# Decoder step with three token mixers on one core: first projection phase in written order with evictions ahead of the next splits, and a new layout of the kernel's end

## Chip, cores, metric

One core of one Trainium2 chip. The metric is the device time of one execution in microseconds (us). Before the change it was 1824.22 us, the median of 3 runs (1823.52 to 1826.77).

## What is computed

One layer of a hybrid decoder is applied to a prompt of 256 positions and to 8 samples of one position each (264 columns in all, width 2048, everything in fp32):

```python
mod = silu(c) @ w_ada + b_ada;  sh1, sc1, gt1, sh2, sc2, gt2 = split(mod, 6)
h = rmsnorm(x, g_pre_mix) * (1 + sc1) + sh1
z = h @ w_in                      # u, v, HGRN2 and GLA inputs, branch gates
...                               # three mixers, gated merge -> merged
x = x + gt1 * rmsnorm(merged @ w_out, g_post_mix)
h2 = rmsnorm(x, g_pre_mlp) * (1 + sc2) + sh2
y2 = square(relu(h2 @ w_mlp_up)) @ w_mlp_down
x = x + gt2 * rmsnorm(y2, g_post_mlp)
```

## The kernel before

**Splits.** Activations and weights are split into a rounded high part and a rest. Each product of a 128x128 weight tile with the 264 columns is three matmuls (L659, L660, L661): high weights times high x, high weights times low x, low weights times high x. `split` (L108) makes the parts of a weight half-tile: ScalarE casts (`whi`, L109), VectorE subtracts (`wlo`, L106). A **granule** (L649) is the work on one item of the weight stream, 8 weight tiles in the first phase, so 24 matmuls. The stream loads items on SyncE's queue (L616, L609; 4 raw buffers) up to five ahead, and `ahead()` splits up to two items ahead of the granule in work; `granule` calls it when its matmuls have been written.

**First phase** (L809 to L844). x has 16 blocks of 128 rows (k). `CHUNKS = (2, 2, 4, 4, 4)` deals them out in five **k steps**, numbered 0 to 4 here. Each k step runs over all twenty 256-column pieces of u, v, q, f and i (`begin`): in k steps 0 and 1 a granule has two pieces (accumulators acc0 and acc1 in PSUM, 12 matmuls each) and there are ten granules, 0 to 9; later there are twenty of one piece. When a granule is done, its accumulators are evicted: copied to SBUF by ScalarE in k step 0 (L825), added to what lies there by VectorE in the others (L827). There are two accumulator buffers, so a granule's acc0 needs the eviction of the last granule's acc0, and acc1 that of acc1.

**What runs ahead.** While k step c runs, `First.paced` loads the columns of `w_ada` that make the shift and scale of k step c+1, on GpSimd's queue (L488; sixteen loads, of 256 KB in k step 0 and of 512 KB after), and spreads their small matmuls (`ada`, L308) behind granules 3 to 6 or so. ScalarE copies the sums (L312), TensorE transposes them, VectorE adds the bias into `mod` (L509) and makes `A1` (L515). Then `modulate` (L439) forms x * A1 + shift: for the samples' 16 columns on VectorE (L451, L452), on GpSimd for the first blocks alone (L445); for the prompt, of each two blocks the first on VectorE (L456), the second on ScalarE (L458). The result is split (`split_tokens`, L121) into the high and low x that the next k step's matmuls read.

**Order.** In the first phase, TensorE, SyncE and GpSimd run in written order (`manual_schedule`, L807); VectorE's and ScalarE's instructions are put in order by the framework's scheduler. Every engine carries out its own list in order, so an instruction that waits holds up all behind it.

**The end** (L1637 to L1710). The last product of the MLP, its eighth column pair (m = 7, L1638 to L1653), goes into both halves of one accumulator. `gated` (L1413) squares it for the norm and multiplies by the gate; four transposes bring it to token order (L851) and two copies (L1447, L1448) put it into the output rows `yt`. Three of the eight 128x512 output pieces are made on TensorE (`by_pe`, L1671): x1 times the identity (L1681), then yt times a diagonal of the norm factors (L1690), both into one accumulator, read out by ScalarE (L1696). The sums of squares (`norms`, L1463, L1464) stand behind two of the L1681 matmuls. A square root on ScalarE (L228) and five small VectorE operations (L229 to L233) give the norm factors `r3`. VectorE makes the other five pieces (L1698). The samples' rows take two VectorE operations (L1703, L1704), a transpose, a copy and a store on ScalarE's queue (L1709). Stores of pieces alternate between SyncE's and ScalarE's queues.

Of the kernel before, what the change touches and what calls it, by code (L numbers as in the profile page):

```python
# [10 lines left out]
AF = mybir.ActivationFunctionType  # L11
# [46 lines left out]
def hybrid_step_kernel(  # L58
# [40 lines left out]
    def mul(o, a, b):  # L99
        V.tensor_tensor(o, a, b, op=ALU.mult)  # L100

    def add(o, a, b):
        V.tensor_tensor(o, a, b, op=ALU.add)  # L103
# [335 lines left out]
    def modulate(dst, src, xs, k0, n, A, B, hi, lo):  # L439

        d = dst[:, :, NP:NT]
        one = k0 == 0
        if one:
            Q = nc.gpsimd
            Q.tensor_tensor(d, xs[:, k0:k0 + n, :], A[:, k0:k0 + n, 1:NC], op=ALU.mult)  # L445
            Q.tensor_tensor(d, d, B[:, k0:k0 + n, 1:NC], op=ALU.add)
            hs, ls = (apart(b)[:, :, :, NP // 2:NT // 2] for b in (hi, lo))
            Q.tensor_copy(hs, by_two(d))
            Q.tensor_tensor(ls, by_two(d), hs.bitcast(F32), op=ALU.subtract)
        else:  # L450
            mul(d, xs[:, k0:k0 + n, :], A[:, k0:k0 + n, 1:NC])  # L451
            add(d, d, B[:, k0:k0 + n, 1:NC])  # L452
        for j in range(n):
            k = k0 + j
            if j % 2 == 0:
                V.tensor_scalar(dst[:, j, 0:NP], src[:, j, :], A[:, k, 0:1], B[:, k, 0:1], ALU.mult, ALU.add)  # L456
            else:
                S.activation(dst[:, j, 0:NP], src[:, j, :], AF.Identity, scale=A[:, k, 0:1], bias=B[:, k, 0:1])  # L458
            if one:
                p = by_two(dst[:, j:j + 1, 0:NP])  # L460
                h, l = (apart(b[:, j:j + 1, :])[:, :, :, 0:NP // 2] for b in (hi, lo))
                if j == 0:
                    V.tensor_copy(h, p)
                    sub(l, p, h.bitcast(F32))
                else:
                    split(p, h, l)
            elif j % 2 == 1:
                js = slice(j - 1, j + 1)
                split_tokens(dst[:, js, :], hi[:, js, :], lo[:, js, :])
# [176 lines left out]

    stream = []

    def granule(w, k0, n, c0, width, accs, xh, xl, k, first, last):  # L649

        item, parts = stream[0].next()
        assert item[1:] == (k0 + k, n, c0, width)
        h = n // 2
        for acc0, m0 in [(acc, 2 * i) for i, acc in enumerate(accs)]:
            for j in range(n):
                for m in range(m0, min(m0 + 2, width // P)):
                    o = acc0[:, m % 2, 0:NT]
                    a, b = (p[:, j % h, m * P:(m + 1) * P] for p in parts[j // h])
                    T.matmul(o, a, xh(k + j), start=first and j == 0, stop=False)  # L659
                    T.matmul(o, a, xl(k + j), start=False, stop=False)  # L660
                    T.matmul(o, b, xh(k + j), start=False, stop=last and j == n - 1)  # L661
        stream[0].ahead()

    levels, samples = [], []
# [138 lines left out]
    stream[0].split_half(0)  # L803
    for k, ps in zip((4, 6), early):
        x_transposed(k, ps)
    order.__exit__(None, None, None)
    order = tc.manual_schedule(engines=set(every[0:3]))  # L807
    order.__enter__()
    k0 = 0  # L809
    for ci, n in enumerate(CHUNKS):  # L810
        final = ci == len(CHUNKS) - 1
        gn = 4 // n
        ng = len(begin) // gn
        if not final:
            nxt = First(k0 + n, CHUNKS[ci + 1]).paced(ng)
        for gi in range(ng):
            if ci or gi:
                accs = [new_acc() for _ in range(gn)]
            else:
                next(nxt)  # L820
            granule(win, 0, n, begin[gi * gn][0], gn * CW, accs, hH, hL, k0, True, True)
            for acc, (c0, dst, fn) in zip(accs, begin[gi * gn:gi * gn + gn]):
                z = acc[:, :, 0:NT]
                if ci == 0:
                    S.copy(dst, z)  # L825
# [810 lines left out]

    def down(f, ah, al):  # L1637
        for m in range(8):  # L1638
            z = linear(w_mlp_down[0], f * (FB // P), FB // P, m * CW, CW, ah, al)
            dst = pair(y2[m // 2], m % 2)  # L1640
            if f == 0:
                S.copy(dst, z)
            elif f < NFB - 1 or m < 7:
                add(dst, dst, z)
            else:
                for i in range(2):
                    add(dst[:, i, :], dst[:, i, :], z[:, i, :])
            if f == NFB - 1:
                g = gated(m, dst, G2)
                if m < 7:  # L1650
                    later.append((now[0], lambda m=m, g=g: put_rows(m, to_tokens(g), yt)))
                else:
                    return g  # L1653

    zs = begin_up()
    order.__exit__(None, None, None)
# [3 lines left out]
    for f in range(NFB):  # L1660
        nxt = up(f + 1) if f + 1 < NFB else None
        if f == NFB - 1:
            rounds.drain()
            mul(G2, mod[:, 5 * KT:6 * KT, :], gpost2T.unsqueeze(2).to_broadcast([P, KT, NC]))
            yt = [[blk([P, 1024]) for _ in range(2)] for _ in range(2)]
        g = down(f, *pend)
        pend = nxt

    by_pe = [(0, 1, 0), (1, 1, 0), (1, 0, 0)]  # L1671
    acc = new_acc()
    sums_pe = {}

    def piece(rows, t, hf, c0):
        return rows[t][hf][:, c0:c0 + 512]

    pt = to_tokens(g)
    for i, p in enumerate(by_pe):
        sums_pe[p] = acc[:, i, :] if i < 2 else sm()  # L1680
        T.matmul(sums_pe[p], ident, piece(x1, *p), start=True, stop=False, skip_group_check=True)  # L1681
        if i == 1:
            r3 = norms()
    put_rows(7, pt, yt)
    r3s = r3[:, 2:2 + NS]
    dg = tmp([P, 2, P], "vt")
    for t in range(2):
        S.activation(dg[:, t, :], ident, AF.Copy, scale=r3[:, t:t + 1])
    for p in by_pe:
        T.matmul(sums_pe[p], dg[:, p[0], :], piece(yt, *p), start=False, stop=True, skip_group_check=True)  # L1690
    for t in range(2):
        for hf in range(2):
            for c0 in (0, 512):
                y = piece(yt, t, hf, c0)
                if (t, hf, c0) in by_pe:
                    S.copy(y, sums_pe[t, hf, c0])  # L1696
                else:
                    V.scalar_tensor_tensor(y, y, r3[:, t:t + 1], piece(x1, t, hf, c0), ALU.mult, ALU.add)  # L1698
                eng = nc.sync if c0 else nc.scalar
                eng.dma_start(y_prompt[0, t * P:(t + 1) * P, hf * 1024 + c0:hf * 1024 + c0 + 512], y)  # L1700
            if t == 0 and hf == 0:
                ys = tmp([P, NS, KT], "sqs", 1)
                mul(gs, gs, r3s.unsqueeze(1).to_broadcast([P, KT, NS]))  # L1703
                add(ys.rearrange("p b k -> p k b"), gs, xsT)  # L1704
                ps = sm([P, P])
                T.transpose(ps, ys.rearrange("p b k -> p (b k)"), ident)
                yo = tmp([P, P], "xsn", 1)
                S.copy(yo, ps)
                nc.scalar.dma_start(y_sample.rearrange("b o (k p) -> (b o k) p", p=P), yo)  # L1709
    order.__exit__(None, None, None)  # L1710


# [45 lines left out]
```

## Time and profile before

| | |
|---|---|
| runs, median (lowest to highest) | 1824.22 us (1823.52 to 1826.77) |
| profiled execution | 1827.14 us |
| its span | 1825.4 us, granted clock 0.996 |
| TensorE busy | 98% of the span |
| VectorE, ScalarE, GpSimd busy | 65%, 55%, 7% |
| HBM | 241 GB/s over the span |

The span is the stretch between the first and last recorded instruction; 1.7 us of the profiled execution lie around it. A timeline row gives start, duration, engine, line, operation and tiles, and in brackets how long the engine had been idle and what it was released by. A row of waits gives engine, tile and line, the releaser, then total us, number and longest. A matmul's record (0.28 us) is longer than the distance between two matmuls, since they are pipelined. "PEld" is the loading of weights, "SPq", "ACTq" and "POOLq" the issuing of DMAs.

### The profile page before, as it was taken

Reading aid. Unit: us, or ns where it says so; the run is one execution under the profiler, and the core shown is the slowest. Engines: PE = TensorE matmul, PEld = TensorE weight load, DVE = VectorE, ACT = ScalarE, POOL = GpSimd, SP = SyncE. Lnnn points to the kernel's source line nnn. Section 1 sums busy time; section 2 is a strip of 40 time slices with the busy share of each in tenths; the row PEclk is TensorE's granted clock in tenths of the full one; section 3 lists DMA queues with packets and bytes.
Section 4 is the critical chain, followed back from the end, with each engine's and each line's share of the span. In section 5 each row is a group of like instructions: output and inputs, shape, how many; then the busy total and the mean of one; then the engine's idle time right before and its main releaser. Section 6 shows DMA issues by size and latency. Waiting matters only on the chain.

```text
span 1825.4 us, 42105 instructions
## 1 busy us (share of the span) xinstructions
PE 1780.2 (98%) x16964; PEld 1690.1 (93%) x16964; DVE 1181.2 (65%) x2092; ACT 1001.2 (55%) x1827; POOL 132.3 (7%) x211
## 2 busy tenths in 40 slices
PE   6999999999999999999999999999999999999998
PEld 4889999989989998989999989999999999999997
DVE  4566677787677696566555667555666666666666
ACT  5444364676766766655444666554554545454554
POOL 4221100102101111210000000000000000000000
PEclk9999999999999999999999999999999999999999
DMA  9999687688788789897988954777666666666663
GB/s 317 360 332 313 197 300 236 210 257 284 239 283 261 236 271 299 264 326 244 305 252 266 330 167 153 250 255 221 196 197 196 196 194 196 193 196 196 196 197 106
DMA packets 330179, 442.05 MB, mean 242 GB/s; under 512 B 14946, under 2 KB 276944, under 8 KB 329984
## 3 DMA queue, kind: packets, MB, share of 16 engines
q1 hardware_dynamic: 311728, 380.26, 65.1%
q0 software_dynamic: 17184, 57.85, 9.1%
q8 instruction: 133, 2.18, 0.5%
q10 hardware_dynamic: 1072, 1.25, 0.2%
q14 instruction: 62, 0.51, 0.1%
HBM read 427.60 MB, written 11.70 MB: 241 GB/s over the span
## 4 chain that ended last, share of the span: by engine, by line
PE 87%; DMA 2%; DVE 2%; issue 2%; ACT 1%; POOL 0%; DVEq 0%; ACTq 0%; POOLq 0%
PE mm L659 27%; PE mm L661 26%; PE mm L660 26%; PE ada L376 3%; DMA vbc<-vs_d 1%; PE ada L308 1%; DVE wlo L106 1%; PE sm L851 1%; DMA raw<-in_w_in_dram 1%; PE sm L679 1%; PE sm L686 0%; DVE b L106 0%; PE sm L1575 0%; DMA st<-in_state_hgrn_dram 0%; DVE b L100 0%
## 5 line engine op out<-in xcount | busy, mean ns | idle before, releaser
L659 PE MATMUL mm<-b,whi 128*128 128x264 f32 x4624 | 1292.7, 280 | 11.7 <-ACT b L825 3.6
L661 PE MATMUL mm<-b,wlo 128*128 128x264 f32 x4624 | 1279.4, 277 | 5.3 <-DVE wlo L106 5.0
L660 PE MATMUL mm<-b,whi 128*128 128x264 f32 x4624 | 1278.8, 277 | 1.9 <-issue 1.1
L106 DVE TENSOR_TENSOR wlo<-raw,whi 128x512 fp32r<-128x512 f32 x1136 | 774.5, 690 | 487.7 <-ACT whi L109 475.8
L109 ACT CAST whi<-raw 128x512 fp32r<-128x512 f32 x1136 | 691.4, 616 | 645.7 <-DVE wlo L106 332.0
L659 PEld LDWEIGHTS mm<-b,whi 128*128 128x128 f32 x4624 | 876.0, 189 | 53.9 <-issue 26.6
L661 PEld LDWEIGHTS mm<-b,wlo 128*128 128x128 f32 x4624 | 876.0, 189 | 7.1 <-DVE wlo L106 7.1
L660 PEld LDWEIGHTS mm<-b,whi 128*128 128x128 f32 x4624 | 876.3, 190 | 2.9 <-issue 1.2
L103 DVE TENSOR_TENSOR b<-b,mm 128x528 f32<-128x528 f32 (+1 forms) x137 | 95.7, 699 | 24.5 <-PE mm L661 12.9
L1106 DVE SCALAR_TENSOR_TENSOR st<-vbc,b,st 128x128 f32<-128x128 f32 (+1 forms) x96 | 34.2, 391 | 52.7 <-DMA vbc<-vs_d 47.5
L1104 ACT ACTIVATE st<-st,fs 128x128 f32<-128x128 f32 (+1 forms) x96 | 37.0, 429 | 46.3 <-DMA st<-in_state_hgrn_dram 27.8
L488 POOL DMA_DIRECT2D b<-in_w_ada_dram x64 | 46.3, 726 | 126.9 <-PE ada L308 94.4
L376 PE MATMUL ada<-araw,cT 128*32 128x512 f32 x296 | 39.8, 601 | 0.0
L308 PE MATMUL ada<-b,cT 128*32 128x256 f32 (+1 forms) x640 | 34.6, 351 | 2.7 <-DMA b<-in_w_ada_dram 2.5
L100 DVE TENSOR_TENSOR b<-b,b 128x512 f32<-128x512 f32 (+1 forms) x47 | 34.0, 744 | 1.3 <-ACT b L1218 1.0
L1107 POOL DMA_DIRECT2D out_dram<-st x32 | 23.6, 737 | 131.7 <-DVE st L1106 131.6
L308 PEld LDWEIGHTS ada<-b,cT 128*32 128x32 f32 x640 | 17.6, 112 | 14.7 <-DMA b<-in_w_ada_dram 6.3
L376 PE MATMUL ada<-b,cT 128*32 128x512 f32 x216 | 26.2, 593 | 0.0
L106 DVE TENSOR_TENSOR b<-gt,b 128x528 fp32r<-128x528 f32 x32 | 22.8, 712 | 3.2
L106 DVE TENSOR_TENSOR b<-b 128x1024 f32<-128x1024 f32 (+1 forms) x24 | 24.4, 1019 | 0.0
L1629 ACT ACTIVATE b<-vt 128x528 fp32r<-128x528 f32 x32 | 22.9, 717 | 1.0
L106 DVE TENSOR_TENSOR b<-b,b 128x1056 fp32r<-128x1056 f32 (+3 forms) x21 | 20.9, 993 | 4.0 <-ACT b L109 3.9
(343 smaller groups left out, 844.6 us busy)
## 6 DMA issues: line engine op xcount, KB each, us to landing
raw<-in_w_in_dram SPq DMA_DIRECT2D x231, 512.0 KB, 4.9
raw<-in_w_mlp_up_dram SPq DMA_DIRECT2D x128, 512.0 KB, 3.9
raw<-in_w_mlp_down_dram SPq DMA_DIRECT2D x128, 512.0 KB, 3.7
araw<-in_w_ada_dram SPq DMA_DIRECT2D x74, 512.0 KB, 5.9
b<-in_w_ada_dram SPq DMA_DIRECT2D x54, 512.0 KB, 6.6
b<-in_w_ada_dram POOLq DMA_DIRECT2D x48, 512.0 KB, 8.6
raw<-in_w_branch_dram SPq DMA_DIRECT2D x48, 512.0 KB, 4.6
raw<-in_w_out_dram SPq DMA_DIRECT2D x32, 512.0 KB, 5.4
```

The source lines that it names most:

```text
L100: V.tensor_tensor(o, a, b, op=ALU.mult)
L103: V.tensor_tensor(o, a, b, op=ALU.add)
L106: V.tensor_tensor(o, a, b, op=ALU.subtract)
L109: S.copy(hi, src)
L308: T.matmul(acc[32 * j:32 * j + 32, 0:n], cT[:, k, :], w[:, n * j:n * j + n], start=k == 0, stop=k == KT - 1)
L376: T.matmul(self.acc[32 * j:32 * j + 32, :], cT[:, k, :], ws[j // 2][:, j % 2 * 512:j % 2 * 512 + 512], start=k == 0, stop=k == KT - 1)
L488: queue.dma_start(w[:, i], w1[k * P:(k + 1) * P, :, self.k0 * P:(self.k0 + self.n) * P])
L659: T.matmul(o, a, xh(k + j), start=first and j == 0, stop=False)
L660: T.matmul(o, a, xl(k + j), start=False, stop=False)
L661: T.matmul(o, b, xh(k + j), start=False, stop=last and j == n - 1)
L1104: S.activation(st[:, i, :], st[:, i, :], AF.Copy, scale=fs[:, h0 + i, b:b + 1])
L1106: V.scalar_tensor_tensor(st[:, i, :], v[:, i, :], k[:, h0 + i, NP + b:NP + b + 1], st[:, i, :], ALU.mult, ALU.add)
```

## The change

Three things. In the first phase all five engines run in written order, and a function `evict` is called for each accumulator as soon as its last matmul is written, so ahead of the next item's splits; in k step 0 acc0 goes through ScalarE and the last accumulator of the granule through VectorE. `modulate` puts the samples' columns on GpSimd for every k step, and from the second pair of blocks on both blocks of the prompt on ScalarE. The end is written anew, for all engines in written order.

```diff
@@ modulate
+        Q = nc.gpsimd
+        Q.tensor_tensor(d, xs[:, k0:k0 + n, :], A[:, k0:k0 + n, 1:NC], op=ALU.mult)
+        Q.tensor_tensor(d, d, B[:, k0:k0 + n, 1:NC], op=ALU.add)
...
-        else:
-            mul(d, xs[:, k0:k0 + n, :], A[:, k0:k0 + n, 1:NC])
-            add(d, d, B[:, k0:k0 + n, 1:NC])
...
-            if j % 2 == 0:
+            if one and j % 2 == 0:
@@ first phase
-    order = tc.manual_schedule(engines=set(every[0:3]))
...
-            granule(win, 0, n, begin[gi * gn][0], gn * CW, accs, hH, hL, k0, True, True)
-            for acc, (c0, dst, fn) in zip(accs, begin[gi * gn:gi * gn + gn]):
+            todo = begin[gi * gn:gi * gn + gn]
+            def evict(acc):
+                c0, dst, fn = todo.pop(0)
                 z = acc[:, :, 0:NT]
-                if ci == 0:
+                if ci:
+                    add(dst, dst, z)
+                elif todo:
                     S.copy(dst, z)
                 else:
-                    add(dst, dst, z)
+                    V.tensor_copy(dst, z)
                 if final and fn is not None:
                     S.activation(dst, dst, fn)
+            granule(win, 0, n, begin[gi * gn][0], gn * CW, accs, hH, hL, k0, True, True, evict)
@@ end
+    last_tile(0)
+    add(sqacc, sqacc, sq[:, 0, :])
+    last_tile(1)
+    pt, ps = sm([P, 2, CW]), sm([P, 2 + NS])
+    last_transposes(0)
+    row_sums(ps, sqacc, True)
+    row_sums(ps, sq[:, 1, :], False)
+    r3 = tmp([P, 2 + NS], "nr", 1)
+    rstd_sqrt(ps, 1.0 / D, r3)
+    last_transposes(1)
     sums_pe = {}
     for i, p in enumerate(by_pe):
-        sums_pe[p] = acc[:, i, :] if i < 2 else sm()
+        sums_pe[p] = new_acc()[:, 0, :] if i < 2 else sm()
         T.matmul(sums_pe[p], ident, piece(x1, *p), start=True, stop=False, skip_group_check=True)
...
     for t in range(2):
         S.activation(dg[:, t, :], ident, AF.Copy, scale=r3[:, t:t + 1])
+    for t in range(2):
+        S.copy(yt[t][1][:, c7], pt[:, t])
...
+    Q.tensor_tensor(gs[:, 14:16, :], dst[:, :, NP:NT], G2[:, 14:16, 1:NC], op=ALU.mult)
+    ys = tmp([P, NS, KT], "sqs", 1)
+    Q.tensor_tensor(gs, gs, r3[:, 2:2 + NS].unsqueeze(1).to_broadcast([P, KT, NS]), op=ALU.mult)
+    Q.tensor_tensor(ys.rearrange("p b k -> p k b"), gs, xsT, op=ALU.add)
+    by_vector(0, 0, 0)
+    by_products(by_pe[0])
+    ps = sm([P, P])
+    T.transpose(ps, ys.rearrange("p b k -> p (b k)"), ident)
+    yo = tmp([P, P], "xsn", 1)
+    S.copy(yo, ps)
+    nc.scalar.dma_start(y_sample.rearrange("b o (k p) -> (b o k) p", p=P), yo)
+    by_products(by_pe[1])
+    by_products(by_pe[2])
+    for p in ((0, 0, 512), (0, 1, 512), (1, 0, 512), (1, 1, 512)):
+        by_vector(*p)
```

`last_tile(i)` computes one half (i = 0, 1) of the last column pair with 24 matmuls into an accumulator of its own, adds it to `y2`, squares it on ScalarE and multiplies by the gate on VectorE. `row_sums` are the matmuls with ones of `norms`, once for `sqacc` (everything up to half 0) and once for the square of half 1, into the same sums. `by_vector` makes a piece with one VectorE operation and stores it on SyncE's queue; `by_products` makes one with the diagonal matmul and a ScalarE copy and stores it on ScalarE's queue.

TensorE's order is otherwise the same as before, and SyncE's has the same loads in the same order; VectorE's and ScalarE's lists differ in the first phase and at the end alone. Three places follow.

ScalarE in k step 0, behind the first granules; `mm` are the accumulators of two granules, two each, `whi` the casts of the next items. Before:

```order
L825 COPY b_171<-mm_441 128x528
L109 CAST whi_467<-raw_394 128x512
L109 CAST whi_471<-raw_394 128x512
L825 COPY b_171<-mm_442 128x528
L825 COPY b_172<-mm_494 128x528
L109 CAST whi_520<-raw_396 128x512
L109 CAST whi_524<-raw_396 128x512
L825 COPY b_172<-mm_495 128x528
```

and now:

```order
L826 COPY b_171<-mm_438 128x528
L109 CAST whi_466<-raw_391 128x512
L109 CAST whi_470<-raw_391 128x512
L826 COPY b_172<-mm_491 128x528
L109 CAST whi_519<-raw_393 128x512
L109 CAST whi_523<-raw_393 128x512
L299 COPY b_529<-sm_530 128x2x256
L826 COPY b_173<-mm_542 128x528
```

The copy of each granule's acc1 stood behind two casts of the next item; it has gone to VectorE (L828, ahead of the `wlo` there), and the copy of the next granule's acc0 still stands behind those casts.

GpSimd between the `w_ada` loads of k step 0 (256 KB each) and those of k step 1 (512 KB each). Before:

```order
L488 DMA b_539<-in_w_ada_dram 128x2x256 x2
L488 DMA b_542<-in_w_ada_dram 128x2x256 x2
L488 DMA b_932<-in_w_ada_dram 128x2x512
L488 DMA b_934<-in_w_ada_dram 128x2x512
L488 DMA b_936<-in_w_ada_dram 128x2x512
```

and now:

```order
L485 DMA b_539<-in_w_ada_dram 128x2x256 x2
L444 TENSOR_TENSOR b_273<-xsn_132,A_169 128x2x8
L445 TENSOR_TENSOR b_273<-b_273,mod 128x2x8
L485 DMA b_929<-in_w_ada_dram 128x2x512
L485 DMA b_931<-in_w_ada_dram 128x2x512
L485 DMA b_933<-in_w_ada_dram 128x2x512
```

The samples' two operations of the modulation, which read `A1`, now stand ahead of all loads for the k step after next; the same holds at each later change of k step.

TensorE at the end, behind the last 128x264 matmul; `a_2232` is `sqacc`, `vt` first the square of half 1 and then the diagonals. Before:

```order
L851 MATMUL sm_24404<-cst,gt_24395 128x128 x4
L1681 MATMUL mm_24403<-b_13648,cst 128x512
L1681 MATMUL mm_24403<-b_13650,cst 128x512
L1463 MATMUL sm_24411<-cst,a_2232_13655 128x1 x2
L1464 MATMUL sm_24411<-a_2232_13655,cst 128x8
L1681 MATMUL sm_24424<-b_13649,cst 128x512
L1690 MATMUL mm_24403<-b_23762,vt_24428 128x512
```

and now:

```order
L1710 MATMUL sm_24402<-cst,gt_24344 128x128 x2
L1705 MATMUL sm_24403<-cst,a_2232_13652 128x1 x2
L1706 MATMUL sm_24403<-a_2232_13652,cst 128x8
L1705 MATMUL sm_24403<-cst,vt_24343 128x1 x2
L1706 MATMUL sm_24403<-vt_24343,cst 128x8
L1710 MATMUL sm_24402<-cst,gt_24344 128x128 x2
L1725 MATMUL mm_24423<-b_13645,cst 128x512
L1725 MATMUL mm_24425<-b_13647,cst 128x512
L1725 MATMUL sm_24427<-b_13646,cst 128x512
L1742 MATMUL mm_24423<-b_23759,vt_24429 128x512
```

All three x1 matmuls moved behind the sums for the norm, and half of the transposes and of the sums wait for half 0 alone.

More of the change, by code (lines that the diff above doesn't have):

```diff
@@ L647, in hybrid_step_kernel, with granule @@
     stream = []
-    def granule(w, k0, n, c0, width, accs, xh, xl, k, first, last):
+    def granule(w, k0, n, c0, width, accs, xh, xl, k, first, last, done=None):
         item, parts = stream[0].next()
@@ L1665, in hybrid_step_kernel @@
             yt = [[blk([P, 1024]) for _ in range(2)] for _ in range(2)]
-        g = down(f, *pend)
+        last = pend
+        down(f, *pend)
         pend = nxt
+    while later:
+        later.pop(0)[1]()
+    order.__exit__(None, None, None)
+    order = tc.manual_schedule(engines=set(every))
+    order.__enter__()
     by_pe = [(0, 1, 0), (1, 1, 0), (1, 0, 0)]
-    acc = new_acc()
-    sums_pe = {}
     def piece(rows, t, hf, c0):
         return rows[t][hf][:, c0:c0 + 512]
-    pt = to_tokens(g)
+    ah, al = last
@@ new lines, in row_sums, with last_transposes @@
+    def row_sums(ps, v, first):
+        for t in range(2):
+            T.matmul(ps[:, t:t + 1], v[:, t * P:(t + 1) * P], ones[:, 0:1], start=first and t == 0, stop=False, skip_group_check=True)
+        T.matmul(ps[:, 2:2 + NS], ones, v[:, NP:NT], start=False, stop=not first, skip_group_check=True)
+    def last_transposes(i):
+        for t in range(2):
+            T.transpose(pt[:, t, i * P:(i + 1) * P], g[:, i, t * P:(t + 1) * P], ident)
+    last_tile(0)
+    add(sqacc, sqacc, sq[:, 0, :])
```

71 lines of the change are left out of this document (34 added, 37 removed).

## The prediction

> **What bounds the kernel now.** I read the page first, then TensorE's waits in the stretch where the change acts first (27 to 260 us), then the timeline at the two ends of the program.
>
> ```profile
> span 1825.4 us, 42105 instructions
> PE 1780.2 (98%) x16964; PEld 1690.1 (93%) x16964; DVE 1181.2 (65%) x2092; ACT 1001.2 (55%) x1827; POOL 132.3 (7%) x211
> ```
>
> TensorE is the bound, and the change leaves its matmuls as they are. So it can win only where TensorE stands still or where the program ends, and every wait that it adds for TensorE is lost in full. The waits, each with total, number and longest:
>
> ```profile
> PE mm L659 <- ACT b L825: 3.6, 5, 2.0
> PE mm L659 <- DVE b L103: 2.1, 3, 1.2
> PE mm L659 <- ACT b L109: 1.5, 1, 1.5
> ...
> PE mm L660 <- DVE b L106: 0.7, 2, 0.4
> ```
>
> The first two rows are the evictions of k steps 0 and 1, the other two the new x of k step 2. A stall is dearer than its idle time:
>
> ```profile
> 40.76 0.38 PE L659 MATMUL mm<-b,whi 128*128 128x264 f32 x1 [1.95 <-ACT b L825]
> ...
> 40.97 0.28 PE L660 MATMUL mm<-b,whi 128*128 128x264 f32 x1
> ...
> 1809.83 0.28 PE L660 MATMUL mm<-b,whi 128*128 128x264 f32 x1
> 1809.94 0.28 PE L661 MATMUL mm<-b,wlo 128*128 128x264 f32 x1
> ```
>
> Undisturbed matmuls start 0.11 us apart (last two rows), yet a record is 0.28 long, so 0.17 ahead of a wait counts as busy; behind it the next one comes 0.21 later, 0.10 more than usual. So each stall costs 0.27 beside its idle time. The eight evictions: 3.6 + 2.1 + 8 x 0.27 = 7.9 us.
>
> **The change, part by part.**
>
> *Evictions, k steps 0 and 1.* Why they are late:
>
> ```profile
> 39.07 1.14 ACT L109 CAST whi<-raw 128x512 fp32r<-128x512 f32 x2 [2.77 <-DMA raw<-in_w_in_dram]
> ...
> 40.11 1.09 ACT L825 COPY b<-mm 128x528 f32<-128x528 f32 x2
> ...
> 43.17 1.14 ACT L109 CAST whi<-raw 128x512 fp32r<-128x512 f32 x2 [1.97 <-DMA raw<-in_w_in_dram]
> ...
> 44.71 0.59 ACT L299 COPY b<-sm 128x512 f32<-128x512 f32 x1
> 44.86 0.38 PE L659 MATMUL mm<-b,whi 128*128 128x264 f32 x1 [0.70 <-ACT b L825]
> ```
>
> ScalarE stands at a cast whose raw weights have not landed, and the copies are queued behind it. The new order takes the copy of acc1 from there, but ScalarE's new rows show the copy of the next acc0 still behind the same two casts. Walked through with the rows above: the stall of 1.95 in granule 2 goes, so it ends near 40.2; granule 3 then needs acc0's copy, which runs from 40.2 (casts 39.07 + 1.14) for 0.55: 0.55 lost. Its acc1 comes from VectorE behind a subtraction: 0.27. Granule 4's acc0 waits for the casts (43.17 + 1.14 = 44.3), the L299 copy that now stands ahead of it and its own copy, some 0.5 each: 45.35, where TensorE is ready at 44.0, so 1.35. One more such place, granule 9, I put at 0.4. Together 2.6, and with 0.1 for each of four short stalls 3.0. In k step 1 the additions now stand ahead of the subtractions, and I count nothing there; if one stalls as before it costs up to 1.2. So 3.0 instead of 7.9: **-4.9**, bounds 0 (the stalls move with the raw loads) and -7.9.
>
> *Modulation for k step 2.*
>
> ```profile
> 110.63 0.67 ACT L109 CAST b<-b 128x528 fp32r<-128x528 f32 x1 [0.21 <-DVE b L456]
> ...
> 111.34 0.38 PE L659 MATMUL mm<-b,whi 128*128 128x264 f32 x1 [1.48 <-ACT b L109]
> ```
>
> TensorE loses 1.5 + 0.7 + 3 x 0.27 = 3.0 here. The samples' operations leave VectorE, and the first prompt block moves from VectorE to ScalarE, which now does two blocks ahead of its cast. One of them is added on ScalarE, one wait between engines is dropped. I take 2.5 left: **-0.5**, bounds -3.0 (all gone) and +0.7 (one cast's length more). At later changes of k step TensorE waited for nothing here, since no such row is in the list.
>
> *Loads of w_ada.* GpSimd's new rows put the two samples' operations, which need `A1`, ahead of all sixteen 512 KB loads. What that moves:
>
> ```profile
> 43.88 0.72 POOL L488 DMA_DIRECT2D b<-in_w_ada_dram  x1 [0.56 <-DMA b<-in_w_ada_dram]
> ...
> 60.85 0.17 DVE L515 SCALAR_TENSOR_TENSOR A<-mod,vec 128x18 f32<-128x18 f32 x1
> ...
> 96.78 1.93 PE L308 MATMUL ada<-b,cT 128*32 128x256 f32 x32
> ```
>
> The loads began at 43.88; now the first waits for `A1` (60.85 before, about as late after) and issues near 61.2. They are needed by the last `ada` matmuls of k step 1: 96.78 before, their last matmuls end at 98.7; the last load has the last 8 of these 32 matmuls, which start half a us sooner; less the 4.9 and with some allowance, 92.9 at the latest. What the DMA gives, from the window 44 to 60 (mean GB/s last in its row) and its queues:
>
> ```profile
> 44.00:60.00 16.00, 15.11 (x223) 14.11 (x222) 6.14 (x10) 9.75 (x19) 8.54 (x12) 1.00 1.03 403
> ...
> q0 software_dynamic: 1163, 4.12, 64.6%
> q1 hardware_dynamic: 1189, 2.29, 38.2%
> ```
>
> The stretch was full at 403 GB/s, GpSimd's loads (q0) at 4.12 MB / 16 = 257, the weights (q1) at 143. Sixteen loads are 8.39 MB, and some nine items of `w_in` are read meanwhile, 4.7 MB: 13.1 MB at 405 GB/s take 32.4 us, so the last lands near 61.2 + 0.9 + 32.4 = 94.5, **+1.6** late. Bounds: 0 (at 270 GB/s for q0 it is in time) and +11 (q0 has half of 403: 8.39 MB / 0.201 = 41.7, landing at 104). I take the middle since the one row of both queues side by side gives q0 more than half. Behind this on GpSimd's queue are only further loads. In k steps 2 and 3 a step has twenty granules for the same sixteen loads, some 53 us instead of 27: cost nothing, covered by that time.
>
> ```profile
> 27.22 0.22 POOL L446 TENSOR_TENSOR b<-b,mod 128x16 f32<-128x16 f32 x1
> 27.65 0.43 DVE L106 TENSOR_TENSOR b<-b,b 128x256 fp32r<-128x256 f32 x1
> 27.78 0.38 POOL L449 TENSOR_TENSOR b<-b,b 128x16 fp32r<-128x16 f32 x1
> ...
> 61.15 0.41 DVE L456 TENSOR_SCALAR b<-b,A,mod 128x256 f32<-128x256 f32 x1
> 61.47 0.17 DVE L103 TENSOR_TENSOR b<-b,mod 128x16 f32<-128x16 f32 x1
> ```
>
> The two added GpSimd operations per pair of blocks cost 0.22 each alone and 0.38 beside a VectorE operation, where 0.17 on VectorE did before; their result is one of the inputs of the split, and the prompt's block (0.41 on VectorE) covers the first of them.
>
> *The end.* Before, in order:
>
> ```profile
> 1810.25 0.77 DVE L103 TENSOR_TENSOR b<-b,mm 128x264 f32<-128x264 f32 x2 [1.87 <-PE mm L661]
> ...
> 1810.78 0.42 ACT L1421 ACTIVATE vt<-b 128x264 f32<-128x264 f32 x1 [2.86 <-DVE b L103]
> ...
> 1812.14 1.88 PE L1681 MATMUL mm<-b,cst 128*128 128x512 f32 x4
> ...
> 1814.69 0.27 ACT L228 ACTIVATE nr<-sm,eps 128x10 f32<-128x10 f32 x1 [1.98 <-PE sm L1464]
> ...
> 1815.94 1.42 DVE L1698 SCALAR_TENSOR_TENSOR b<-b,nr,b 128x512 f32<-128x512 f32 x2
> ...
> 1816.45 1.98 PE L1690 MATMUL mm<-b,vt 128*128 128x512 f32 x4 [0.90 <-ACT vt L1688]
> ...
> 1818.47 1.07 ACT L1696 COPY b<-mm 128x512 f32<-128x512 f32 x2 [1.78 <-PE mm L1690]
> ...
> L1700 ACTq DMA_DIRECT2D out_dram<-b x4: 375/428/746, 1816.7 to 1820.9; - x4
> ...
> DMA to landing us min/median/max: 2.3/2.7/3.4
> ```
>
> The last matmul starts at 1809.94; the square root comes 4.75 later, because the sums stand behind two x1 matmuls (four records in 1.88). Now half 0 is done earlier, its sums too, and half 1 needs one addition (to 1810.7), one square (to 1811.2) and the sums (to about 1812.0): the root at 1812.1, 2.59 earlier. Behind it the root and the five small operations are the same, so the first VectorE piece starts at 1813.35 instead of 1815.94. TensorE is next: three x1 matmuls of 0.86 to 0.94 now stand behind the sums, from 1812.1 to 1814.7, and the first product at 1814.7 instead of 1816.45, 1.75 earlier. ScalarE reads the pieces out as they come and stores them, with the samples' store between; its last issue I put at 1818.45 instead of 1820.9. Five pieces on VectorE at 0.71 end at 1816.9. Last landing: 1818.45 + 2.7 = 1821.15, where before it was 1820.9 + 2.7 = 1823.6: **-2.4**. Bounds: -1.0 (only TensorE's products count and ScalarE's added store and copy cost 0.7) and -2.7 (all that the root gains). The samples on GpSimd:
>
> ```profile
> 1089.79 0.43 POOL L1530 TENSOR_TENSOR gs<-gs,nr 128x128 f32<-128x128 f32 x1 [1.27 <-DVE nr L233]
> 1090.31 0.46 POOL L1531 TENSOR_TENSOR xsT<-xsT,gs 128x128 f32<-128x128 f32 x1
> ```
>
> 0.43 + 0.46 from 1813.4 end at 1814.3, ahead of the transpose that stands behind the first product, so they cost nothing; if each is held up by a VectorE piece of 0.71, the transpose is late by 0.3 and TensorE with it: -2.1. The Trainium skill, page "SBUF — State Buffer", section "Who interferes with whom", says that a VectorE operation with two SBUF inputs and a GpSimd one that touches SBUF exclude each other, the later one blocking in full; the 0.38 beside 0.43 above agrees in kind. By it the sum below would be -5.9 instead of -6.2.
>
> **Sum.** -4.9 - 0.5 + 1.6 - 2.4 = -6.2. On the profiled execution (1827.14: the span and 1.7 around it) that is 1820.9. It lies 2.9 above the median of the runs shown, 1824.22, and I apply the same difference to the median: **1818.0**.
>
> **Rivals.**
>
> *A. The weights' arrival is the bound in k steps 0 and 1, chance 0.18.* For it: ScalarE's casts waited 2.77 and 1.97 for raw weights in the rows above. Then an eviction sooner makes the next cast the wait, and only the end is won: 1824.22 - 2.4 = 1821.8. Against it: the list has stalls on evictions eight times, and between 44 and 60 the loads of w_ada, which filled the DMA, are gone now.
>
> *B. The loads of w_ada come late, chance 0.12.* One mechanism: they issue behind the modulation at 61.2 instead of 43.88, and TensorE, whose order is fixed, stands before the last `ada`. All else brings -7.8. By 61.2 + 0.9 + 8.39 MB / rate, less 92.9, the gain is used up below 217 GB/s and the kernel is slower by 0.2% (3.65 us) below 198. At 190 GB/s the load lands at 106.3, 13.4 late: 1824.2 - 7.8 + 13.4 = 1829.8. For it: the weights' own need during granules of 24 x 0.11 = 2.66 us is 524 KB each, 197 GB/s, so that q0 could be left with 206. Against it: q0's 257 above. The Trainium skill, page "DMA: Bandwidth & Descriptors", section "Queues, rings and completion order", has each DMA engine go round its queues packet by packet, which would give q0 half, 11 us late and about 1827; the row of 64.6% to 38.2% does not agree.
>
> *C. Everything is won, chance 0.10.* No eviction stalls, the new x is in time, the loads too: -7.9 - 3.0 - 2.7 = -13.6 at most; with a part of it 1812 to 1814.
>
> That the change does not do what it says is excluded by the rows of the order.
>
> **How the numbers follow.** The forecast holds 0.60, A 0.18, B 0.12, C 0.10. Range: from 1812.5 (C's middle) to 1825 (A with its end at -1.0 or B at the rate where it has used up the gain), leaving out the worse part of B and a tail of C. A measurement can tell some 0.2% from no change, 3.65 us: 1820.6 and 1827.9. Faster: the forecast but for its upper end (0.57) and C, so 0.67. Same: A, that end and half of B's milder part, 0.23. Slower: the rest of B, 0.10.
>
> **What would show it.** In the profile after: waits of the first matmul line (then L656) for L826 of about 2.6 in all, at granules 3 and 4, and none for the additions of k step 1. First 512 KB load of w_ada issued near 61, last `ada` of k step 1 waiting 1 to 2 us; over 8 means B. The change to k step 2 with 2 to 3 us of waits. At the end, first VectorE piece 3.4 us behind the last 128x264 matmul instead of 6.0, last store issued 8.5 behind it instead of 11.0. The prediction is wrong if casts take over the waits (A), if the loads stall TensorE in k steps 2 and 3, where I see cover, or if the last store's landing grows because the stores come closer together.

## The result

| | before | after |
|---|---|---|
| runs, median (lowest to highest), 22 each | 1826.63 us (1823.52 to 1832.14) | 1822.45 us (1819.63 to 1827.23) |
| ratio, 95% interval | | 0.9979 (0.9973 to 0.9985) |
| profiled execution, its span | 1827.14, 1825.4 | 1821.87, 1820.0 |

The change makes the kernel faster by 0.21%, that is 3.8 us (2.7 to 4.9). The forecast was 6.2. The three runs known at the time (median 1824.22) lay low: over 22 runs the kernel before takes 1826.63, so the point forecast of 1818.0 started 2.4 too low. The gain was 2.4 too large by the ratio, 2.0 by the medians. By number the result is nearest to rival A, where only the end is won (1821.8). That is chance: A's mechanism is not what the profile shows, as the sections below work out.

### The profile page after: what moved, and what is told of

The parts are those of the page before. It is cut to its first block, busy times and chain, and to the rows that moved or that the text cites. A ratio compares the mean times of both kernels' runs of the same rounds, so it can differ in the third digit from the quotient of the medians.

```text
span 1820.0 us, 42083 instructions
## 1 busy us (share of the span) xinstructions
PE 1780.2 (98%) x16970; PEld 1689.8 (93%) x16970; DVE 1178.7 (65%) x2077; ACT 996.9 (55%) x1824; POOL 136.9 (8%) x228
## 4 chain that ended last, share of the span: by engine, by line
PE 88%; DVE 2%; issue 2%; DMA 1%; ACT 1%; POOL 0%; ACTq 0%; DVEq 0%; POOLq 0%
PE mm L656 27%; PE mm L658 26%; PE mm L657 26%; PE ada L376 3%; DMA vbc<-vs_d 1%; PE ada L308 1%; PE sm L854 1%; DVE wlo L106 1%; PE sm L678 1%; PE sm L685 0%; DVE b L106 0%; PE sm L1578 0%; PE sm L1209 0%; DMA st<-in_state_hgrn_dram 0%; ACT whi L109 0%
## 5 line engine op out<-in xcount | busy, mean ns | idle before, releaser
L103 DVE TENSOR_TENSOR b<-b,mm 128x528 f32<-128x528 f32 (+1 forms) x137 | 95.4, 698 | 63.3 <-PE mm L658 55.6
L1109 DVE SCALAR_TENSOR_TENSOR st<-vbc,b,st 128x128 f32<-128x128 f32 (+1 forms) x96 | 34.2, 392 | 52.4 <-DMA vbc<-vs_d 45.9
L376 PE MATMUL ada<-araw,cT 128*32 128x512 f32 x296 | 40.7, 601 | 0.0
L376 PE MATMUL ada<-b,cT 128*32 128x512 f32 x216 | 26.2, 593 | 0.0
```

The lines of the kernel that those rows point to most:

```text
L376: T.matmul(self.acc[32 * j:32 * j + 32, :], cT[:, k, :], ws[j // 2][:, j % 2 * 512:j % 2 * 512 + 512], start=k == 0, stop=k == KT - 1)
L1109: V.scalar_tensor_tensor(st[:, i, :], v[:, i, :], k[:, h0 + i, NP + b:NP + b + 1], st[:, i, :], ALU.mult, ALU.add)
```

## The profile after

TensorE's waits in the first phase, from 27 to 260 us, as for before (engine, tile, line, releaser, then total, number, longest):

```profile
PE ada L308 <- DMA b<-in_w_ada_dram: 3.5, 3, 1.3
PE mm L656 <- ACT b L826: 1.7, 3, 0.8
PE mm L656 <- ACT whi L109: 0.8, 1, 0.8
PE mm L656 <- DVE b L103: 0.7, 1, 0.7
PE mm L656 <- POOL b L448: 0.4, 1, 0.4
```

The evictions, 5.7 us idle in eight stalls before (one of them, 0.24, at the change to k step 2), take 1.7 in three (L826); the one wait on an L103 addition, 0.7, is now at the change to k step 2. The wait of 1.5 on ScalarE's cast there is gone. A new row stands on top: `ada` waits for its loads three times. These are GpSimd and the `ada` matmuls in the timeline:

```profile
58.82 0.21 POOL L444 TENSOR_TENSOR b<-xsn,A 128x16 f32<-128x16 f32 x1 [16.65 <-DVE A L512]
59.11 0.22 POOL L445 TENSOR_TENSOR b<-b,mod 128x16 f32<-128x16 f32 x1
59.60 5.78 POOL L485 DMA_DIRECT2D b<-in_w_ada_dram  x8 [0.27 <-PE mm L658]
```

```profile
76.27 1.93 PE L308 MATMUL ada<-b,cT 128*32 128x256 f32 x32
81.03 1.93 PE L308 MATMUL ada<-b,cT 128*32 128x256 f32 x32
85.80 1.50 PE L308 MATMUL ada<-b,cT 128*32 128x256 f32 x24
88.17 0.64 PE L308 MATMUL ada<-b,cT 128*32 128x256 f32 x8 [0.88 <-DMA b<-in_w_ada_dram]
91.64 1.16 PE L308 MATMUL ada<-b,cT 128*32 128x256 f32 x16
94.08 0.64 PE L308 MATMUL ada<-b,cT 128*32 128x256 f32 x8 [1.28 <-DMA b<-in_w_ada_dram]
96.04 0.64 PE L308 MATMUL ada<-b,cT 128*32 128x256 f32 x8 [1.32 <-DMA b<-in_w_ada_dram]
```

GpSimd idles 16.65 us for `A1` and issues the first load at 59.6. The `ada` groups come every 4.76 us while nothing is late, so the fourth would end at 76.27 + 3 x 4.76 + 1.93 = 92.5; it ends at 96.68. **The loads cost 4.2 us.** How full the DMA was is the last number of these windows (first the stretch, its length, busy time of PE, PEld, DVE, ACT and POOL, clock, DMA share, GB/s):

```profile
44.00:61.00 17.00, 17.00 (x242) 16.35 (x243) 9.91 (x18) 9.53 (x18) 1.84 (x4) 1.00 0.76 256
...
80.00:96.00 16.00, 12.56 (x146) 8.70 (x145) 8.78 (x14) 3.68 (x7) 0.72 (x1) 1.00 1.04 408
```

Where it ran at 403 GB/s before it now runs at 256, and the loads that are missing there are what TensorE waits for at 88 to 96.

The end, in the order of the forecast's steps:

```profile
1807.21 0.28 PE L1696 MATMUL mm<-b,wlo 128*128 128x264 f32 x1
...
1809.40 0.27 ACT L228 ACTIVATE nr<-sm,eps 128x10 f32<-128x10 f32 x1 [0.99 <-PE sm L1706]
...
1810.64 3.78 DVE L1738 SCALAR_TENSOR_TENSOR b<-b,nr,b 128x512 f32<-128x512 f32 x5
...
1810.75 0.93 POOL L1748 TENSOR_TENSOR gs<-gs,nr 128x128 f32<-128x128 f32 x1 [2.50 <-DVE nr L233]
...
1811.76 0.79 POOL L1749 TENSOR_TENSOR sqs<-gs,xsT 128x128 f32<-128x128 f32 x1
...
1812.84 0.27 PE L1753 MATMUL sm<-cst,sqs 128*128 128x128 f32 x1
...
1813.04 0.58 ACT L1743 COPY b<-mm 128x512 f32<-128x512 f32 x1 [1.12 <-PE mm L1742]
...
1814.11 0.27 ACT L1755 COPY xsn<-sm 128x128 f32<-128x128 f32 x1 [0.48 <-PE mm L1742]
...
1814.84 0.58 ACT L1743 COPY b<-mm 128x512 f32<-128x512 f32 x1 [0.46 <-PE sm L1742]
...
1816.45 0.34 ACTq L1734 DMA_DIRECT2D out_dram<-b  x1
```

Behind the start of the last 128x264 matmul the square root comes 2.19 us later (4.75 before), the first VectorE piece 3.43 (6.00) and the last store 9.24 (10.96).

**How far two profiles can be compared.** Instructions that are the same in both traces give the shift at each place. It is -0.6 ahead of the first granule, with nothing changed there. And the granted clock differs (the last number but two):

```profile
27.00:34.00 7.00, 5.36 (x27) 4.78 (x28) 5.55 (x11) 5.42 (x11) 6.78 (x13) 0.76 0.73 247
```

```profile
27.00:34.00 7.00, 5.74 (x43) 5.13 (x44) 5.67 (x11) 6.21 (x13) 6.92 (x11) 1.00 0.79 251
```

Before (first row) had half the clock for 3.4 us in granule 0, after (second row) had not; the shift grows there from -0.62 to -1.86. Neither belongs to the change. Below, shifts against before are corrected for both: less the shift ahead of granule 0, and 1.24 added where a run has no half clock near 30 us. With that, executions of like order still differ by about 1 us in the first phase: e1 below, whose first phase is that of before, stands at +0.5. Further on, from 311 to 1085 us, where the edits change nothing, the shifts of the experiments move by between -3.0 (e3) and +2.0 (e6), so a total can't be read from one trace.

## The experiments

Times are ratios to the kernel before in the same session; us are of 1827.

**e1, the end alone.**

```diff
+        last = pend
+        down(f, *pend)
...
+    last_tile(0)
+    add(sqacc, sqacc, sq[:, 0, :])
+    last_tile(1)
...
```

> The kernel before with the new end alone. Theory: the end gives 2.3 us by itself (in the trace after, the shift against before grows from -3.1 ahead of the last tile to -5.4 at the end), so -2.3 us against before, last VectorE piece started 3.4 us behind the last 128x264 matmul. Rival: the stores come closer together and the end gains nothing when the rest is not earlier: 0 to -1.

Measured: 0.9992 (0.9983 to 1.0), so -1.5 us (-3.1 to 0). The interval alone does not exclude the rival's 0 to -1; the trace bears the theory out: its shift is +0.97 ahead of the last tile and -1.28 at the end, 2.25 for the end; after has -3.08 and -5.34, e3 -1.27 and -3.52, the same 2.25 each.

**e2, the first phase alone**: the changed kernel with the end of before.

```diff
+            granule(win, 0, n, begin[gi * gn][0], gn * CW, accs, hH, hL, k0, True, True, evict)
...
+        Q.tensor_tensor(d, xs[:, k0:k0 + n, :], A[:, k0:k0 + n, 1:NC], op=ALU.mult)
...
```

> The changed kernel with the old end, so the first phase's changes alone. Theory: evictions -4.4, late loads of w_ada +4.2, change of k step -1.3, sum -1.5 us against before; waits of the ada matmuls for w_ada some 3.5 us idle in k step 1. Rival (the forecast on record was right and one execution misled): -3.8 us.

Measured: 0.9997 (0.9987 to 1.0007), -0.5 us (-2.4 to +1.3). The rival's -3.8 is outside.

```profile
PE ada L308 <- DMA b<-in_w_ada_dram: 2.6, 2, 1.3
PE mm L656 <- ACT b L826: 1.7, 2, 1.5
```

The same waits as in after, idle times a little shorter (27 to 260 us). So the first phase's changes, for which the forecast had -3.8, bring next to nothing. e1 and e2 add up to -2.0, with intervals wide enough for the -3.8 of the whole change.

**e3, the loads early, the new order**: the samples' columns on VectorE again.

```diff
-        Q.tensor_tensor(d, xs[:, k0:k0 + n, :], A[:, k0:k0 + n, 1:NC], op=ALU.mult)
-        Q.tensor_tensor(d, d, B[:, k0:k0 + n, 1:NC], op=ALU.add)
+        E = Q if one else V
+        E.tensor_tensor(d, xs[:, k0:k0 + n, :], A[:, k0:k0 + n, 1:NC], op=ALU.mult)
+        E.tensor_tensor(d, d, B[:, k0:k0 + n, 1:NC], op=ALU.add)
```

> The changed kernel with the samples' columns of the modulation on VectorE again (GpSimd for k step 0 alone, as before), so that the w_ada loads are not held behind A1. Theory: the ada matmuls of k step 1 no longer wait, 4.2 us come back: -8 us against before, -4.2 against the changed kernel; first 512 KB load issued near 42 to 44. Rival (the DMA is full in k step 1 whatever the order, since evictions alone brought the need 6 us forward): waits for w_ada or for raw weights stay, gain below 1 us against the changed kernel.

Measured: 0.9997 (0.9987 to 1.0006), -0.5 us. **A miss for the theory as I had it.** No `ada` of k step 1 waits, yet the evictions do (27 to 260 us):

```profile
PE mm L657 <- DVE b L103: 3.8, 4, 1.4
PE mm L657 <- ACT b L827: 1.9, 2, 1.5
PE mm L657 <- ACT b L109: 1.2, 1, 1.2
PE mm L658 <- DVE b L106: 1.1, 3, 0.4
```

That is 5.7 us again on evictions (L103 and L827), as before the change, though every eviction is written ahead of the next splits. By their places, 4.3 of it lie in five stalls up to 79 us (before: 5.5 in seven) and 1.4 is an addition at the change to k step 2. The five go mostly with the weights. The two queues from 44 to 60 us (packets, MB, share of the 16 engines):

```profile
q0 software_dynamic: 1168, 4.13, 65.0%
q1 hardware_dynamic: 1167, 2.24, 37.4%
```

The packets are shared one for one, but in the trace's list of packets q0's data are in packets of 4096 bytes (1007, and 161 packets of 4 bytes) and q1's, the weights', in packets of 2048 (1094, and 73 of 4 bytes). The weights get 2.24 MB / 16 = 140 GB/s where TensorE wants 197 (524 KB for each granule of 2.66 us), the casts wait for them, and evictions queue behind the casts and subtractions:

```profile
67.90 1.14 ACT L109 CAST whi<-raw 128x512 fp32r<-128x512 f32 x2 [1.58 <-DMA raw<-in_w_in_dram]
68.55 1.29 DVE L106 TENSOR_TENSOR wlo<-raw,whi 128x512 fp32r<-128x512 f32 x2 [0.77 <-ACT whi L109]
```

In e3 six casts between 45.9 and 68 us waited for weights; in after, none between the one at 45.3 and the one at 70.2. That the shared packets are the reason is argued from these rows: no run here changes the share alone.

The weights are not the whole of the miss. With the samples on VectorE in written order, their two operations stand behind the subtractions of weights, and ScalarE's cast of the new x waits for them, at the change to k step 2 and again at the next:

```profile
109.50 0.66 ACT L109 CAST b<-b 128x528 fp32r<-128x528 f32 x1 [1.52 <-DVE b L446]
...
172.77 0.70 ACT L109 CAST b<-b 128x528 fp32r<-128x528 f32 x1 [0.91 <-DVE b L446]
```

At the changes to k steps 3 and 4, where the shift of after does not move, e3's grows by 0.85 and 0.83 us (e5's by 0.84 and 0.82). So e3 is not simply the changed kernel with early loads: of the 8 us expected, 1.7 are lost there.

**e4, the loads held, the old order.**

```diff
         else:
-            mul(d, xs[:, k0:k0 + n, :], A[:, k0:k0 + n, 1:NC])
-            add(d, d, B[:, k0:k0 + n, 1:NC])
+            Q = nc.gpsimd
+            Q.tensor_tensor(d, xs[:, k0:k0 + n, :], A[:, k0:k0 + n, 1:NC], op=ALU.mult)
+            Q.tensor_tensor(d, d, B[:, k0:k0 + n, 1:NC], op=ALU.add)
```

> The kernel before with the samples' columns on GpSimd for all k steps and nothing else, so the loads are held but the evictions are as late as before. Theory (need and arrival race): the loads land near 97.5 to 98.5, the last ada matmuls need the last one at 98.1, so 0 to +1.5 us against before. Rival (holding the loads costs its own price wherever it is): +4.2 us.

Measured: 1.0004 (0.9995 to 1.0013), +0.7 us (-0.9 to +2.4). Its first load issues at 61.32, later than in after, and still no `ada` waits, since TensorE arrives late by itself:

```profile
81.54 1.93 PE L308 MATMUL ada<-b,cT 128*32 128x256 f32 x32
...
95.83 1.93 PE L308 MATMUL ada<-b,cT 128*32 128x256 f32 x32
```

So holding the loads has no price of its own here. Corrected shifts in us (first `ada` of k step 1, ahead of the late loads, and the addition behind granule 1 of k step 2, where loads and modulation are in):

| | first `ada` of k step 1 | k step 2 |
|---|---|---|
| old order, loads early (before) | 0 | 0 |
| old order, loads held (e4) | -1.0 | -1.5 |
| new order, loads early (e3) | -1.6 | -1.1 |
| new order, loads held (after) | -4.4 | -1.5 |

These are single executions, but other runs repeat three of the rows: at the first `ada`, e1 (as before) has +0.5, e5 (as e3, loads cut in two) -1.9, e2 (as after) -4.3. The evictions' gain needs both, the new order and the loads held back; and with the loads held it is paid back ahead of k step 2.

**e5, smaller packets.**

```diff
-                queue.dma_start(w[:, i], w1[k * P:(k + 1) * P, :, self.k0 * P:(self.k0 + self.n) * P])
+                for r in range(2 if self.k0 == 4 else 1):
+                    if self.k0 == 4:
+                        queue.dma_start(w[:, i, r], w1[k * P:(k + 1) * P, r, self.k0 * P:(self.k0 + self.n) * P])
+                    else:
+                        queue.dma_start(w[:, i], w1[k * P:(k + 1) * P, :, self.k0 * P:(self.k0 + self.n) * P])
```

> The kernel of e3 (samples on VectorE, loads not held) with each 512 KB load of w_ada for k step 2 cut into two DMAs of 256 KB with rows of 2 KB. Theory (the two queues take packets in turn, one for one, and w_ada's 4096-byte packets against the weights' 2048 starve the weights): if the packets become 2048 bytes, both get about 200 GB/s, the waits on evictions fall from 5.7 us (e3, L103 and L827) to under 3, and the last ada of k step 1 still has its data: 2 to 3 us earlier at k step 2 than e3. If the packets stay 4096 bytes, as e3. Rival (the evictions are late for the order of the instructions, not for the weights): as e3 whatever the packets.

Measured: 0.9985 (0.9976 to 0.9994), -2.7 us; not told apart from e3. The data packets stayed at 4096 bytes (975 of them, and 243 of 4 bytes), so two rows of 2 KB went in one, the share hardly changed and the experiment says nothing on packets of 2048:

```profile
q0 software_dynamic: 1218, 3.99, 63.3%
q1 hardware_dynamic: 1223, 2.36, 39.3%
```

Corrected shifts -1.9 and -1.4, waits on evictions 5.3 (3.9 of it up to 76 us): as e3.

**e6, four loads ahead.** The changed kernel; `soon` is the `First` of k step 2, made early.

```diff
+            if ci == 0 and gi == 4:
+                for b in range(4):
+                    soon.load(b)
```

> The changed kernel with four of the sixteen w_ada loads for k step 2 issued ahead of the samples' operations on GpSimd, as early as buffers allow (about 43 to 47 us). Theory: 2.1 MB fewer behind 59.6, so the ada of k step 1 no longer waits (+4.2 gone), while the weights of k step 0 are slowed for some 8 us and give back 1 to 2: 2 to 3 us earlier at k step 2 than the changed kernel. Rival (the stretch to k step 2 is full of transfers, so what ada wins the evictions lose): within 1 us of the changed kernel.

Measured: 0.9952 (0.9939 to 0.9966), -8.8 us. Shifts about -4.5 and -5.8 (its half clock, from 26.2 us, reaches into granule 0, which makes them less certain): no `ada` waits in k step 1, and the evictions lose nothing against after, where I had expected 1 to 2.

**e7, four loads at 50 us.**

```diff
+            if gate is not None:
+                queue.tensor_copy(w[:, 0, 0, 0:1], gate)
...
+            if ci == 0 and gi == 5:
+                for b in range(4):
+                    soon.load(b, begin[gi * gn][1][:, 0, 0:1] if b == 0 else None)
```

> As e6, but a GpSimd copy of one element of granule 5's result ahead of the four loads holds them to about 50 us, where in the changed kernel the DMA had gone idle. Theory: the weights of k step 0 are not slowed and ada does not wait: 4 us earlier at k step 2 than the changed kernel, waits on w_ada in k step 1 under 0.5 us, the same waits on evictions as the changed kernel (about 2.4). Rival: as in e6, within 1 us of the changed kernel.

Measured: 0.9946 (0.9932 to 0.996), -9.9 us (-7.3 to -12.4). Shifts -4.8 and -6.1, 4.6 earlier at k step 2 than after. GpSimd's rows and the waits from 27 to 260 us:

```profile
50.64 0.18 POOL L484 COPY b<-b 128x1 f32<-128x1 f32 x1 [8.79 <-ACT b L832]
51.14 2.88 POOL L487 DMA_DIRECT2D b<-in_w_ada_dram  x4 [0.32 <-POOL b L484]
```

```profile
PE mm L658 <- ACT b L832: 1.5, 2, 1.4
PE mm L658 <- ACT whi L109: 0.8, 1, 0.8
PE mm L658 <- DVE b L103: 0.7, 1, 0.7
PE mm L659 <- DVE b L106: 0.4, 1, 0.4
```

The wait on w_ada has left the list, nothing has taken its place. That four loads moved by 8 us win 4.6 us in the trace, more than the 3.8 of the whole change, rules out that the stretch is simply full of transfers.

**e8, k step 4 in the scheduler's order**, on top of e7.

```diff
+        if final:
+            order.__exit__(None, None, None)
+            order = tc.manual_schedule(engines=set(every[0:3]))
+            order.__enter__()
```

> As e7, but with VectorE and ScalarE in the scheduler's order again in k step 4, the last one of the first phase. Theory: the second constant ada group near 258 us, which takes 2.0 us with a pause of 0.8 on a DMA in the changed kernel and 1.06 before, takes 1.06 again: 0.9 us earlier at 300 us than e7; about -7 against before in all. Rival (that pause is a matter of where the transfers happen to stand): no change against e7.

Measured: 0.9945 (0.9933 to 0.9958), median 1817.52, -10.0 us; its interval and e7's are the same. The trace shows the pause. The second constant `ada` group near 258 us, of before, of after, and of e8:

```profile
261.25 1.06 PE L376 MATMUL ada<-araw,cT 128*32 128x512 f32 x8
```

```profile
257.89 2.00 PE L376 MATMUL ada<-araw,cT 128*32 128x512 f32 x8
```

```profile
254.62 1.07 PE L376 MATMUL ada<-araw,cT 128*32 128x512 f32 x8
```

e2 and e7 have the long one too, but e6, in the same written order, has a short one. Counted by the shift from 249 to 273 us, the loss is wider: it grows by 0.3 to 1.0 us in all eight runs whose k step 4 is in written order (after, e2, e3, e5, e6, e7, e9, e10) and by nothing in the three that have the scheduler's there (e1, e4, e8). So the written order costs something in k step 4 each time, about 1.0 us at most, too little for the times of e7 and e8 to show.

**e9 and e10, one load and two at 50 us**, else as e7, one execution each.

```diff
-                for b in range(4):
+                for b in range(1):
```

> As e7 with one load of w_ada ahead instead of four. Theory (arrival and need race): behind 59 us the loads bring 265 GB/s while both queues are full, so 0.524 MB less makes the last ada 2.0 us less late: 4.2 - 2.0 = 2.2 us between its place in an even step and its end in k step 1. Rival (the first loads' start-up is what costs, or any load ahead is enough): 4.2 or 0.

> As e7 with two loads of w_ada ahead. Theory: 4.2 - 4.0 = 0.2 us late, so nearly all of e7's gain. Rival: as in e9.

The last `ada` of e9, and the first and last of e10:

```profile
90.45 1.53 PE L308 MATMUL ada<-b,cT 128*32 128x256 f32 x24
93.23 0.64 PE L308 MATMUL ada<-b,cT 128*32 128x256 f32 x8 [1.25 <-DMA b<-in_w_ada_dram]
```

```profile
77.20 1.93 PE L308 MATMUL ada<-b,cT 128*32 128x256 f32 x32
...
91.48 1.93 PE L308 MATMUL ada<-b,cT 128*32 128x256 f32 x32
```

In e9 the fourth group ends at 93.87 where an even step would end at 92.38: 1.5 late (2.2 expected). In e10 it is on time (91.48 = 77.20 + 3 x 4.76). Lateness by loads ahead: 4.2 with none (after), 1.5 with one, 0 with two, and 0 with four (e7). It is a race between arrival and need, and two loads decide it. The times, 1819.78 and 1818.52 us with 1830.81 for before beside them, are of one execution each and can't tell these two from e7.

## Why the forecast was too large

| step | forecast | measured in the trace | where |
|---|---|---|---|
| evictions, k steps 0 and 1 | -4.9 | -4.4 | first `ada` 82.50 to 76.27, less -0.62 at the start and -1.24 of clock |
| loads of w_ada late | +1.6 | +4.2 | 92.5 to 96.68 |
| change to k step 2 | -0.5 | -1.3 | -2.04 to -3.36 |
| k step 4 | 0 | +0.94 | L376 group, 2.00 for 1.06 |
| the end | -2.4 | -2.25 | -3.08 to -5.34 |
| sum | -6.2 | -2.8 | |

The rest of the span's -5.4 is -0.6 at the start, -1.24 of clock and -0.7 spread over 300 to 850 us, where runs of like order differ by more. The timed -3.8 (2.7 to 4.9) contains -2.8.

**Evictions: right in size, incomplete in cause.** I put the late evictions down to the order, with the missing weights as a second thought (rival A). e3 and e4 show that each alone brings 1 to 1.6, both 4.4. So the size came out right partly by luck: the term had priced the order alone. What is left of the stalls is 1.7 us idle on L826 where I had 2.6, and nothing in k step 1, as forecast. Rival A's other half, that the weights' arrival leaves nothing to gain, fell with e6 and e7: the DMA had room, 256 of some 400 GB/s from 44 to 61.

**Loads: this is the step that failed.** The mechanism was right, named with its place and priced; the term was mis-sized, +1.6 for 4.2. The loads even issued sooner than I assumed (59.6 for 61.2), but three figures were kinder than the trace. The rate: I divided 13.1 MB by 405 GB/s from the first microsecond; the first 5 us gave less (0.93 MB for q0 up to 65 us, then 262 GB/s from 65 to 90), and the last packets straggled until 96, so that the last load came near 95.9 and not at 94.5. The need: the evictions' own gain brings TensorE to the last `ada` at 90.6, its last load is wanted near 92, I had 92.9. And an arrival late by some margin stops TensorE at each of three loads, with a restart each time. The lateness grew by 2.6: 1.4 from the arrival, 0.9 from the need, the rest from the restarts. I had seen the gain and the lateness as two terms to add; they are one race, in which **each us won ahead of the `ada` is lost there again** as long as the loads don't start sooner.

One reading behind it was wrong too. I set the rule of the Trainium skill, page "DMA: Bandwidth & Descriptors", section "Queues, rings and completion order" (each DMA engine goes round its queues packet by packet), against q0's 64.6% to 38.2% and wrote that the row does not agree. The same rows have 1163 packets to 1189, one for one, which agrees with the rule as far as a count can (whether the profile's packets are those of the page, no run here shows). The share in bytes follows the packets' size, which is twice as large on q0. Half of the bytes for q0 was my inference, not the rule's. Read in packets, the rows show that w_ada leaves the weights 143 GB/s while it loads, and that would have pointed to why the evictions were late.

**Modulation: sign right, size small.** The wait of 1.5 on ScalarE's cast went; 0.7 on an addition (L103) came in its place. It took both parts of the edit: e3, with both prompt blocks on ScalarE but the samples on VectorE, still waits 1.2 us for that cast, and so does e4, with only the samples moved.

**k step 4: a cover that wasn't one.** I had counted nothing behind k step 2. SyncE's issue of the constant part of `w_ada` comes at 251.42 in after, 0.2 later than before's 251.21 although all else is 3.4 earlier, and the group of `ada` behind it takes 0.94 longer. e8 shows that the written order of VectorE and ScalarE is the cause; which instruction holds the issue back stays open.

**The end: right in sum, by two errors that cancel.** The root came 2.56 sooner, counted from the last matmul (2.59 forecast). But the last store is issued 9.24 behind that matmul instead of the 8.5 forecast, so 1.72 sooner than before and not 2.45. The step that was too short is ScalarE's: from its copy at 1813.04 its four copies and four issues of stores stand one directly behind another, 3.41 us up to the last issue. The last store then lands 2.5 us after its issue where before it took 3.4; I had 2.7 for both, so that is luck. The last tile itself takes 0.35 longer than before.

The samples on GpSimd cost nothing, as forecast: the second operation ends at 1812.55, and the transpose starts at 1812.84, 0.86 behind the first product (1811.98), as close as two products stand to each other (1812.95 and 1813.81). Beside VectorE's pieces the two operations took 0.93 and 0.79 where I had 0.43 and 0.46, and two of the pieces took 0.92 and 0.94 instead of 0.74. That agrees in kind with the exclusion that the Trainium skill's page "SBUF — State Buffer", section "Who interferes with whom", states for a VectorE instruction with two SBUF inputs and a GpSimd one that reads SBUF. The pieces lost less, some 0.2 each, than the 0.43 and 0.46 of the operations beside them, so these rows don't show that one blocks the other in full. The 0.38 and 0.22 that I had set side by side in the prediction are two different operations, L449 and L446, and showed less than I took from them.

**What stays open.** In e4's trace TensorE is 1.5 us earlier at k step 2, yet its time is 0.9 lower to 2.4 higher than before's; a single execution is not good for less. What sets the half clock of granule 0 is not known, but it is not the edits: e7 to e10 carry out the same instructions up to 50 us, and from 27 to 34 us e8 and e9 have 0.76, e7 and e10 1.00.

## What to carry to other kernels

When an edit makes an engine arrive earlier, look for the transfers that it will meet sooner, and price arrival against need as one race instead of adding a gain and a loss. An operation that waits, placed ahead of DMA issues on the same queue, delays all of them: put a few of the loads ahead of it. Two of sixteen were enough in e10's one execution; four gave 0.9952 (0.9939 to 0.9966) of the kernel before as early as buffers allowed, 0.9946 (0.9932 to 0.996) at 50 us, and 0.9945 (0.9933 to 0.9958) with the scheduler's order in k step 4 besides, three that these intervals don't tell apart, against 0.9979 for the change. Read a queue's share in packets as well as in bytes.

## What had not been expected of the hardware

GpSimd's loads move in packets of 4096 bytes and SyncE's weights in packets of 2048 (e3's list of packets), and with both queues full the packets were shared one for one (1163 to 1189 in before, 1168 to 1167 in e3), so the weights got 143 and 140 of some 400 GB/s. Cutting GpSimd's DMAs to rows of 2 KB left the packets at 4096 (e5: 1218 packets, 3.99 MB). The granted clock fell to half for 3.4 us at places that differ between executions (near 30 us in before, at 96.6 in e2, not at all in the first phase of after). One such stretch moved the profile of before by 1.24 us; at half speed throughout it would be at most 3.4 / 2 = 1.7.
